# Input products of a state-space layer: three 32-row matrix products against one of 128 rows, stacked by way of DRAM

## The chip, the cores and the metric

The kernel runs on one core of one Trainium2 chip. The time is that of the device for one execution, in microseconds (us). Three runs of the kernel before took 2914.17, 2914.20 and 2915.66 us; the median is 2914.2 us.

## The reference: what is computed

The kernel computes two layers of a streaming encoder on 256 tokens of width 2048, in float32. Each layer does this:

```
h  = rms_norm(x) ;  proj = h @ w_in            # latents, u (1024 wide), gate logits
a  = mla(...)                                  # attention, 16 heads, block-causal mask
s  = s5(u, ...)                                # state-space model, 64 groups of 16 inputs and 64 states
x  = x + rms_norm((sigmoid(ga)*a + sigmoid(gb)*s) @ w_out)
x  = x + rms_norm(swiglu(rms_norm(x)))
```

The part that matters here is the entry of the state-space model. A group g has 16 input channels and 64 complex states, and its inputs are turned into state inputs by a small complex matrix:

```
bu_re = einsum('bsgp,gnp->bsgn', u, bb_re)     # (256 tokens, 16 inputs) -> 64 states, per group
bu_im = einsum('bsgp,gnp->bsgn', u, bb_im)
```

A scan over the 256 tokens follows, then the product with C, a skip term, a GELU and a gated linear layer (GLU).

## The kernel before, in words

**Products in two parts.** Tiles of type `F32R` hold one part of a number. Each operand of a big product is split into a high part and a low remainder, and the product is taken as high x high + high x low + low x high: three products where one would do. The big products (`gemm`, lines 448 to 450) do that with 128x128 weights and 512 columns. Each weight tile is loaded by a DMA of the SP queue, copied to its high part by ScalarE (line 187), and VectorE subtracts to get the low part (the tile `lo`, in `Weights.split_to`; its time shows at line 151, a helper through which all VectorE operations pass).

**Main line and background.** The program text goes through the big products of a layer one after the other: input projection (`u`, `ckv`, `cq`, `ga`, `gb`), attention, output projection `wo`, GLU, `out`, feed-forward. Everything else is background, woven in when the program is written: after each group of six matrix products (`bg.step`) the planner runs what has come due (`bg.later`, `bg.chain`: so many steps from now) and then lets the generators in its list go on, as long as the VectorE time that it has counted is less than the counted TensorE time plus a lead. So the order of instructions on each engine is fixed when the program is written. The planner's costs know nothing of how long a DMA takes.

**The state-space model (generator `s5`)** is background. It works in 32 steps `ct` of two groups each, four steps to one tile of 128 inputs (`ft`, eight tiles). For each `ft`, `prep` builds the input matrix: four ScalarE copies, two transposes on TensorE, a high part `bd[:, 0]` (ScalarE) and a low part `bd[:, 1]` (VectorE), then the same for C. For each `ct`, `emit_bu` multiplies the 32 rows that belong to its two groups: `bd[r, e, i]` against `uz[r, e, ft]`, where `uz` holds the high and low part of u, transposed. VectorE then takes the result `bu` from PSUM, scans it, and `emit_y` multiplies with C (128 rows, 32 columns). `emit_bu` for the next `ct` is due two steps after VectorE has read the last one. The state-space model starts during the input projection and has to be done when the GLU begins: `begin_glu` runs all background that is left.

**Where bu gets its operands.** Both `bd` and `uz` lie in SBUF in the places where the 32 rows of a `ct` are four different strips of the 128 partitions. `u_ready` tells the generator that half of `uz` is there (entries 1 and 2 are appended eight steps after each of the two products `u`); before `emit_bu` of the next `ct` it waits until the preparation of that `ft` has been issued (`mats[ft][2]`).

**Queues.** Weights, gates and C come by SP's queue. POOL's queue carries, in the kernel before, only the small vectors at the start, the state-space tables of the second layer and the rows of x at the two ends of a layer: nothing while the state-space steps run.

The functions that the change touches are `s5` with `prep`, `emit_bu` and the loop over `ct`, the lines after each product `u`, and the head of the loop over the layers:

Of the kernel before, what the change touches and what calls it, by code (L numbers as in the profile page):

```python
# [10 lines left out]
F32R = mybir.dt.float32r  # L11
# [9 lines left out]
S = 256  # L21
# [199 lines left out]
def trunk_kernel(ctx: ExitStack, tc: tile.TileContext, a: dict, out: bass.AP, cst: bass.AP,  # L221
                 depth: int = 2, tap=None):
    nc = tc.nc
    PE, ACT, SP = nc.tensor, nc.scalar, nc.sync
# [7 lines left out]
    dp = ctx.enter_context(tc.tile_pool(name="dp", bufs=1, space=DRAM))  # L232
# [4 lines left out]
    bg = Background()  # L237
# [3 lines left out]
    def T(pool, shape, tag, dt=F32, **kw):  # L241
        cnt[0] += 1
        return pool.tile(list(shape), dt, tag=tag, name=f"{tag}_{cnt[0]}", **kw)
# [11 lines left out]
    def tt(o, x, y, op):  # L255
        V.tensor_tensor(out=o, in0=x, in1=y, op=op)
# [10 lines left out]
    def act(o, x, f, **kw):  # L267
        ACT.activation(out=o, in_=x, func=f, **kw)  # L268
# [3 lines left out]
    def parts(hi, lo, src):  # L272
        return [lambda: act(hi, src, AF.Copy), lambda: tt(lo, src, hi.bitcast(F32), SUB)]
# [197 lines left out]
    def transpose(o, x, rows=128):  # L471
        PE.transpose(o, x, ident[0:rows, 0:rows])  # L472
# [386 lines left out]
    tab_d, base_d = T(dp, [128, 928], "tab"), T(dp, [128, 2048], "base")  # L859
    prev = ExitStack()  # L860
    for l in range(depth):
        u_ready = []
        h = feat.h
        uz = mp = sp = ap = st = sub = None

# [15 lines left out]
        def s5(l=l, gains=gains):  # L881
# [70 lines left out]
            def load_c(ft):  # L952
                t = T(sp, [128, 2, 2, 64], "craw", bufs=2)
                for i, nm in enumerate(("ssm_c_re", "ssm_c_im")):
                    src = a[nm][l, 8 * ft:8 * ft + 8].rearrange("g p n -> (g p) n")
                    for d in range(2):
                        SP.dma_start(out=t[:, i, d], in_=src)
                return t

            yps = T(ps5, [128, 2, S], "y")  # L960
            mats = {}

            def prep(ft, craw):

                bx = T(sp, [128, 2, 4, 2, 16], "bx")
                for i in range(2):
                    for g in range(2):
                        act(bx[:, i, :, g], bb[:, i, 4 * ft:4 * ft + 4], AF.Copy, scale=gm[g])
                ps = yps[:, ft % 2]
                bd = T(sp, [128, 2, 2, 128], "bd", F32R, bufs=2)  # L970
                cm = T(sp, [128, 2, 4, 2, 16], "cm", bufs=2)

                def tr(srcs):
                    for i in range(2):
                        transpose(ps[:, 128 * i:128 * i + 128], srcs[i])

                def ev_c(i):
                    v = ps[:, 128 * i:128 * i + 128].rearrange("p (c g q) -> p c g q", g=2, q=16)
                    for g in range(2):
                        act(cm[:, i, :, g], v[:, :, g], AF.Copy, scale=gm[2 * i + g])  # L980

                it = bg.chain(2, [
                    lambda: tr([bx[:, i].rearrange("p c g q -> p (c g q)") for i in range(2)]),
                    lambda: None,
                    *parts(bd[:, 0], bd[:, 1], ps.rearrange("p (i n) -> p i n", i=2)),
                    lambda: tr([craw[:, i].rearrange("p d n -> p (d n)") for i in range(2)]),
                    lambda: None, lambda: ev_c(0), lambda: ev_c(1)])
                mats[ft] = (bd, cm, it)

            def emit_bu(ct):  # L990
                ft, c = divmod(ct, 4)
                r = slice(32 * c, 32 * c + 32)
                bd = mats[ft][0]
                bu = T(ps5, [128, 2, S], "bu")
                for i in range(2):
                    o = bu[:, i]
                    uh, ul = uz[r, 0, ft], uz[r, 1, ft]
                    PE.matmul(out=o, lhsT=bd[r, 0, i], rhs=uh, start=True, stop=False)  # L998
                    PE.matmul(out=o, lhsT=bd[r, 1, i], rhs=uh, start=False, stop=False)  # L999
                    PE.matmul(out=o, lhsT=bd[r, 0, i], rhs=ul, start=False, stop=True)  # L1000
                bus[ct] = bu

            def emit_y(ct, xx):
                ft, c = divmod(ct, 4)
                cm = mats[ft][1]
                yo = yps[32 * c:32 * c + 32, ft % 2]
                for i in range(2):
                    PE.matmul(out=yo, lhsT=cm[:, i, c].rearrange("p g q -> p (g q)"), rhs=xx[:, i],  # L1008
                              start=(i == 0), stop=(i == 1))
# [21 lines left out]
            nxt_c = load_c(1)  # L1031
# [4 lines left out]
            e = e_start(0)  # L1036
# [3 lines left out]
                e_add(e, t, 0, k)  # L1040
                yield
            e_mirror(e)
            yield from bg.until(mats[0][2])
            while not u_ready:
                yield
            bu_due = bg.later(1, lambda: emit_bu(0))
            y_due = None
            yield
            for ct in range(NCT):
                ft, c = divmod(ct, 4)  # L1050
                if c == 1 and ft + 1 < 8:
                    prep(ft + 1, nxt_c)
                    if ft + 2 < 8:
                        nxt_c = load_c(ft + 2)
                yield from bg.until(bu_due)
                bu = bus.pop(ct)
                more = ct + 1 < NCT
                if more:
                    en = e_start(ct + 1)
                    et = e_mul(en, ct + 1, 0)  # L1060
                buv = bu.rearrange("p i t -> p t i")
                p1 = T(sp, [128, S, 2], "P", bufs=2)
                tt(p1, e, buv, MUL)
                p2 = T(sp, [128, S, 2], "P", bufs=2)
                tt(p2, e, buv[:, :, ::-1], MUL)
                if more:
                    e_add(en, et, ct + 1, 0)
                yield
                if more:
                    while len(u_ready) < 1 + (ct + 1) // 16:  # L1070
                        yield
                    yield from bg.until(mats[(ct + 1) // 4][2])
                    bu_due = bg.later(2, lambda ct=ct: emit_bu(ct + 1))
                z = T(sp, [128, 2, S], "Z")
                tt(z[:, 0], p1[:, :, 0], p1[:, :, 1], ADD)
                tt(z[:, 1], p2[:, :, 0], p2[:, :, 1], SUB)
                yield
                if more:
                    et = e_mul(en, ct + 1, 1)
                dec = mag[:, ct:ct + 1].to_broadcast([128, S])  # L1080
                for i in range(2):
                    V.tensor_tensor_scan(out=z[:, i], data0=dec, data1=z[:, i], initial=0.0, op0=MUL, op1=ADD)
                yield
                if more:
                    e_add(en, et, ct + 1, 1)
                zz = z.rearrange("p i t -> p t i")
                p3 = T(sp, [128, S, 2], "P", bufs=2)
                tt(p3, e, zz, MUL)
                p4 = T(sp, [128, S, 2], "P", bufs=2)
                tt(p4, e[:, :, ::-1], zz, MUL)  # L1090
                yield
                if more:
                    e_mirror(en)
                if y_due is not None:
                    yield from bg.until(y_due)
                xx = T(sp, [128, 2, S], "xx", bufs=2)
                tt(xx[:, 0], p3[:, :, 0], p3[:, :, 1], SUB)
                tt(xx[:, 1], p4[:, :, 0], p4[:, :, 1], ADD)
                yield
                y_due = bg.later(2 if more else 1, lambda ct=ct, xx=xx: emit_y(ct, xx))  # L1100
                if more:
                    e = en
                if c == 3:
                    g = T(sp, [128, 2, S], "gelu", bufs=1)
                    bg.chain(4 if more else 2, gelu(ft, g), 3 if more else 1)
# [20 lines left out]
        for c in range(2):  # L1126
            def done_u(tb, ps, c=c):
                nonlocal arena, utok
                if arena is None:
                    arena = T(xp, [128, 4096], "X")  # L1130
                    utok = arena[:, 2048:4096].rearrange("p (b n) -> p b n", b=2)
                act(utok[:, tb, 512 * c:512 * c + 512], ps, AF.Copy, scale=rstd[:, tb:tb + 1])

            gemm("u", KD, lhs_of(h), 512, done_u, before=first if c == 0 else None)
            put_pairs(3, uz, 4 * c, lambda c=c: utok[:, :, 512 * c:512 * c + 512])
            bg.later(8, lambda: u_ready.append(1))


        ckvT = T(ap, [128, 2, 2, S], "ckvT", F32R)
# [162 lines left out]
        for p in range(NPAIR):  # L1302
# [33 lines left out]
            for h_ in range(2):  # L1336
                o = kk_ps[:, 256 * h_:256 * h_ + 256]
                e = slice(256 * h_, 256 * h_ + 128)
# [14 lines left out]
            for tb in range(NT):  # L1353
                o = v_ps[:, 256 * tb:256 * tb + 256].rearrange("p (h e) -> p h e", h=2)
# [12 lines left out]
        p = NPAIR - 1  # L1367
# [142 lines left out]
```

## Time and profile before

| | |
|---|---|
| median of three runs | 2914.2 us |
| the profiled execution, its own time | 2915.5 us |
| its span, first to last instruction | 2913.7 us |
| TensorE busy | 2882.4 us (99%) |
| VectorE busy | 1902.1 us (65%) |
| ScalarE busy | 1412.6 us (48%) |
| POOL busy | 33.1 us (1%), 65 instructions |
| moved by DMA | 553.77 MB, mean 190 GB/s |
| mean granted TensorE clock | 0.998 of full speed |

PE is TensorE, PEld its weight loads, DVE VectorE, ACT ScalarE; POOL issues DMAs of its own queue. A matrix product's duration in the trace is from its issue to its last result, and the products overlap: the step from one start to the next is what a product costs the engine. A line such as `32*128 32x256` reads: a weight of 32 rows and 128 columns, and a moving operand of 32 rows and 256 columns.

### The profile page before, as it was taken

Reading aid. Unit: us, or ns where it says so; the run is one execution under the profiler, and the core shown is the slowest. Engines: PE = TensorE matmul, PEld = TensorE weight load, DVE = VectorE, ACT = ScalarE, POOL = GpSimd, SP = SyncE. Lnnn points to the kernel's source line nnn. Section 1 sums busy time; section 2 is a strip of 40 time slices with the busy share of each in tenths; the row PEclk is TensorE's granted clock in tenths of the full one; section 3 lists DMA queues with packets and bytes.
Section 4 is the critical chain, followed back from the end, with each engine's and each line's share of the span. In section 5 each row is a group of like instructions: output and inputs, shape, how many; then the busy total and the mean of one; then the engine's idle time right before and its main releaser. Section 6 shows DMA issues by size and latency. Waiting matters only on the chain.

```text
span 2913.7 us, 37400 instructions
## 1 busy us (share of the span) xinstructions
PE 2882.4 (99%) x13557; PEld 2353.5 (81%) x13557; DVE 1902.1 (65%) x2988; ACT 1412.6 (48%) x2343; POOL 33.1 (1%) x65
## 2 busy tenths in 40 slices
PE   8999999999999999999999999999999999999998
PEld 7777887788788888888877778878878888888887
DVE  7888998775665454444478888976655454544444
ACT  6655665444544444344366556644445444444433
POOL 0000000000000000000010000000000000000000
PEclk9999999999999999999999999999999999999999
DMA  7666335666666566666576663357666666666654
GB/s 225 198 195 190 111 117 177 201 223 205 211 203 212 180 189 200 190 198 199 180 228 193 198 187 112 113 174 240 225 209 209 186 188 195 188 181 231 198 198 145
DMA packets 311221, 553.77 MB, mean 190 GB/s; under 512 B 44352, under 2 KB 57084, under 8 KB 310652
## 3 DMA queue, kind: packets, MB, share of 16 engines
q1 hardware_dynamic: 301708, 528.43, 58.2%
q0 software_dynamic: 4544, 14.42, 1.5%
q10 hardware_dynamic: 4784, 8.53, 0.8%
q8 instruction: 106, 1.74, 0.2%
q14 instruction: 79, 0.65, 0.1%
HBM read 532.74 MB, written 18.56 MB: 189 GB/s over the span
## 4 chain that ended last, share of the span: by engine, by line
PE 96%; DVE 2%; DMA 1%; ACT 1%; issue 0%; DVEq 0%; ACTq 0%
PE acc L448 28%; PE acc L449 28%; PE acc L450 28%; PE y L1008 2%; PE aux L472 2%; PE bu L998 1%; PE acc L1313 1%; PE acc L1314 1%; PE acc L1315 1%; DVE lo L151 1%; DMA xo<-x 1%; PE bu L999 1%; DVE X L151 1%; PE bu L1000 1%; PE aux L1293 1%; PE aux L1244 0%
## 5 line engine op out<-in xcount | busy, mean ns | idle before, releaser
L151 DVE TENSOR_TENSOR lo<-raw,hi 128x1024 fp32r<-128x1024 f32 (+3 forms) x992 | 1147.2, 1171 | 604.0 <-PE acc L449 392.4
L187 ACT ACTIVATE hi<-raw 128x1024 fp32r<-128x1024 f32 (+3 forms) x992 | 993.8, 1019 | 731.3 <-PE acc L450 556.3
L448 PE MATMUL acc<-hi,H 128*128 128x512 f32 (+1 forms) x2432 | 965.3, 397 | 0.6 <-ACT hi L187 0.3
L450 PE MATMUL acc<-hi,H 128*128 128x512 f32 (+1 forms) x2432 | 945.6, 389 | 4.4 <-DVE H L151 4.2
L449 PE MATMUL acc<-lo,H 128*128 128x512 f32 (+1 forms) x2432 | 946.2, 389 | 1.1 <-DVE lo L151 0.9
L448 PEld LDWEIGHTS acc<-hi,H 128*128 128x128 f32 x2432 | 457.5, 188 | 108.9 <-issue 13.2
L450 PEld LDWEIGHTS acc<-hi,H 128*128 128x128 f32 x2432 | 457.6, 188 | 103.8 <-DVE H L151 8.8
L449 PEld LDWEIGHTS acc<-lo,H 128*128 128x128 f32 x2432 | 458.0, 188 | 89.4 <-DVE lo L151 2.5
L448 PE MATMUL acc<-hi,aT 128*128 128x512 f32 x704 | 274.4, 390 | 0.0
L449 PE MATMUL acc<-lo,aT 128*128 128x512 f32 x704 | 274.1, 389 | 0.0
L450 PE MATMUL acc<-hi,aT 128*128 128x512 f32 x704 | 274.1, 389 | 0.0
L448 PEld LDWEIGHTS acc<-hi,aT 128*128 128x128 f32 x704 | 132.2, 188 | 27.6
L449 PEld LDWEIGHTS acc<-lo,aT 128*128 128x128 f32 x704 | 132.2, 188 | 27.4
L450 PEld LDWEIGHTS acc<-hi,aT 128*128 128x128 f32 x704 | 132.2, 188 | 27.1
L448 PE MATMUL acc<-hi,uz 128*128 128x512 f32 x256 | 101.2, 396 | 1.6 <-ACT uz L268 1.6
L268 ACT ACTIVATE X<-acc,rstd 128x512 f32<-128x512 f32 (+1 forms) x64 | 41.2, 650 | 122.0 <-PE acc L450 119.5
L448 PE MATMUL acc<-hi,mT 128*128 128x512 f32 x256 | 100.2, 391 | 0.0
L449 PE MATMUL acc<-lo,uz 128*128 128x512 f32 x256 | 100.0, 390 | 0.2 <-DVE lo L151 0.2
L450 PE MATMUL acc<-hi,uz 128*128 128x512 f32 x256 | 99.8, 390 | 0.0
L450 PE MATMUL acc<-hi,mT 128*128 128x512 f32 x256 | 99.7, 390 | 0.0
L449 PE MATMUL acc<-lo,mT 128*128 128x512 f32 x256 | 99.7, 389 | 0.0
L268 ACT ACTIVATE aT<-aux 128x512 fp32r<-128x512 f32 x44 | 26.1, 599 | 146.4 <-PE aux L472 146.4
(194 smaller groups left out, 2707.0 us busy)
## 6 DMA issues: line engine op xcount, KB each, us to landing
raw<-in_w_in_dram SPq DMA_DIRECT2D x176, 512.0 KB, 4.3
raw<-in_w_ffn_gate_dram SPq DMA_DIRECT2D x176, 512.0 KB, 4.2
raw<-in_w_ffn_up_dram SPq DMA_DIRECT2D x176, 512.0 KB, 3.8
raw<-in_w_ffn_down_dram SPq DMA_DIRECT2D x176, 512.0 KB, 4.5
raw<-in_w_o_mla_dram SPq DMA_DIRECT2D x64, 512.0 KB, 4.2
raw<-in_w_glu_dram SPq DMA_DIRECT2D x64, 512.0 KB, 4.8
raw<-in_w_out_dram SPq DMA_DIRECT2D x64, 512.0 KB, 4.7
raw<-in_w_uq_dram SPq DMA_DIRECT2D x32, 384.0 KB, 3.5
```

What stands on the lines that cost most here:

```text
L151: return f(**kw)
L187: self.nc.scalar.activation(out=dst(hv), in_=src(self.raw[n]), func=AF.Copy)
L268: ACT.activation(out=o, in_=x, func=f, **kw)
L448: PE.matmul(out=o, lhsT=xh, rhs=h[:, kk], start=(k == 0), stop=False)
L449: PE.matmul(out=o, lhsT=xh, rhs=lo[:, kk], start=False, stop=False)
L450: PE.matmul(out=o, lhsT=xl, rhs=h[:, kk], start=False, stop=(k == nk - 1))
L472: PE.transpose(o, x, ident[0:rows, 0:rows])
L998: PE.matmul(out=o, lhsT=bd[r, 0, i], rhs=uh, start=True, stop=False)
L999: PE.matmul(out=o, lhsT=bd[r, 1, i], rhs=uh, start=False, stop=False)
L1000: PE.matmul(out=o, lhsT=bd[r, 0, i], rhs=ul, start=False, stop=True)
L1008: PE.matmul(out=yo, lhsT=cm[:, i, c].rearrange("p g q -> p (g q)"), rhs=xx[:, i], start=(i == 0), stop=(i == 1))
L1293: PE.matmul(out=o[:, 256 * h_:256 * h_ + 256], lhsT=t["v"][:, 0, e], rhs=pT[:, h_, 0:256], start=True, stop=False)
```

## The change: what it does

The four blocks of 32 rows that make up a product in two parts are stacked over the 128 partitions: matrix `bs` holds [high, low, high, low] of B, operand `us` holds [high, high, low, low] of u. One product of 128 rows then gives high x high + low x high + high x low + low x low. The stacks are made by way of DRAM: u goes to `u_d` (two DMAs of 512 KB for each half, `put_u`, eight steps after each product `u`), each prepared B goes to `b_d[ft]` (one DMA of 256 KB, `put_b`, a step in the middle of `prep`'s chain), and `load_stacks` reads them back. A stack serves two `ct` (a pair `p`); it takes eight DMAs of 64 KB, four for `bs` and four for `us`, each onto 32 partitions. There are two buffers of each; the stack of pair p+2 is issued when `emit_bu` has used pair p, and no earlier than the `b_d` and `u_d` that it reads. All of these DMAs are issued from POOL. `bd` has one buffer in place of two. `prep(ft + 1)` is called late in the first `ct` of a tile, not at the start of the second. The generator waits for the stack of the next pair to have been issued, not for `mats[ft]`.

```diff
-        u_ready = []
+        u_ready, more_u = [], []
+        u_d = T(dp, [2, 128, 8, S], f"u_d{l}", F32R)
+
+        def put_u(c):
+            for e in range(2):
+                nc.gpsimd.dma_start(out=u_d[e, :, 4 * c:4 * c + 4], in_=uz[:, e, 4 * c:4 * c + 4])
+            u_ready.append(1)
+            for f in more_u:
+                f()
...
-                bd = T(sp, [128, 2, 2, 128], "bd", F32R, bufs=2)
+                bd = T(sp, [128, 2, 2, 128], "bd", F32R)
...
                     *parts(bd[:, 0], bd[:, 1], ps.rearrange("p (i n) -> p i n", i=2)),
+                    lambda: put_b(ft, bd),
...
+            b_d = T(dp, [8, 2, 128, 2 * 128], f"b_d{l}", F32R)
+            stacks, nput = {}, [0]
+
+            def put_b(ft, bd):
+                nc.gpsimd.dma_start(out=b_d[ft].rearrange("e p n -> p e n"), in_=bd.rearrange("p e i n -> p e (i n)"))
+                nput[0] = ft + 1
+                load_stacks()
+
+            def load_stacks():
+                while len(stacks) < 2 + len(used) and len(stacks) < 2 * nput[0] and len(stacks) < 8 * len(u_ready):
+                    p = len(stacks)
+                    ft, c0 = divmod(p, 2)
+                    rows = slice(64 * c0, 64 * c0 + 64)
+                    bs = T(sp, [128, 2, 256], "bs", F32R, bufs=2)
+                    us = T(sp, [128, 2, S], "us", F32R, bufs=2)
+                    for e in range(4):
+                        for dst, src in ((bs, b_d[ft, e % 2, rows]), (us, u_d[e // 2, rows, ft])):
+                            nc.gpsimd.dma_start(out=dst[32 * e:32 * e + 32], in_=src.rearrange("(c r) n -> r c n", r=32))
+                    stacks[p] = (bs, us)
...
             def emit_bu(ct):
-                ft, c = divmod(ct, 4)
-                r = slice(32 * c, 32 * c + 32)
-                bd = mats[ft][0]
+                p, c = divmod(ct, 2)
+                bs, us = stacks[p]
                 bu = T(ps5, [128, 2, S], "bu")
                 for i in range(2):
-                    o = bu[:, i]
-                    uh, ul = uz[r, 0, ft], uz[r, 1, ft]
-                    PE.matmul(out=o, lhsT=bd[r, 0, i], rhs=uh, start=True, stop=False)
-                    PE.matmul(out=o, lhsT=bd[r, 1, i], rhs=uh, start=False, stop=False)
-                    PE.matmul(out=o, lhsT=bd[r, 0, i], rhs=ul, start=False, stop=True)
+                    PE.matmul(out=bu[:, i], lhsT=bs[:, c, 128 * i:128 * i + 128], rhs=us[:, c], start=True, stop=True)
                 bus[ct] = bu
+                if c == 1:
+                    used.append(p)
+                    load_stacks()
...
-            yield from bg.until(mats[0][2])
-            while not u_ready:
+            yield from bg.until(mats[0][1])
+            while not stacks:
                 yield
...
-                if c == 1 and ft + 1 < 8:
-                    prep(ft + 1, nxt_c)
...
-                    while len(u_ready) < 1 + (ct + 1) // 16:
+                    while (ct + 1) // 2 not in stacks:
                         yield
-                    yield from bg.until(mats[(ct + 1) // 4][2])
...
+                if c == 0 and ft + 1 < 8:
+                    prep(ft + 1, nxt_c)
...
-            bg.later(8, lambda: u_ready.append(1))
+            bg.later(8, lambda c=c: put_u(c))
```

## Rows read from the trace of the kernel before

**Rows 1.** The page's first part: busy time, share of the span, instructions.
```profile
PE 2882.4 (99%) x13557; PEld 2353.5 (81%) x13557; DVE 1902.1 (65%) x2988; ACT 1412.6 (48%) x2343; POOL 33.1 (1%) x65
```
**Rows 2.** The chain that ended last, share of the span by engine.
```profile
PE 96%; DVE 2%; DMA 1%; ACT 1%; issue 0%; DVEq 0%; ACTq 0%
```
**Rows 3.** Timeline of PE, one bu block: start, duration, line, tiles, rows*columns.
```profile
109.42 0.39 PE L450 MATMUL acc<-hi,H 128*128 128x512 f32 x1
109.74 0.38 PE L998 MATMUL bu<-uz,bd 32*128 32x256 f32 x1
109.96 0.27 PE L999 MATMUL bu<-uz,bd 32*128 32x256 f32 x1
...
110.42 0.27 PE L1000 MATMUL bu<-uz,bd 32*128 32x256 f32 x1
110.63 0.50 PE L448 MATMUL acc<-hi,H 128*128 128x512 f32 x1
110.96 0.40 PE L449 MATMUL acc<-lo,H 128*128 128x512 f32 x1
111.20 0.39 PE L450 MATMUL acc<-hi,H 128*128 128x512 f32 x1
```
**Rows 4.** Groups by line: busy us, mean ns, and idle time before.
```profile
L151 DVE TENSOR_TENSOR lo<-raw,hi 128x1024 fp32r<-128x1024 f32 (+3 forms) x992 | 1147.2, 1171 | 604.0 <-PE acc L449 392.4 <-ACT hi L187 145.2 <-issue 59.6
L998 PE MATMUL bu<-uz,bd 32*128 32x256 f32 x128 | 42.1, 329 | 0.0
```
**Rows 5.** Timeline of PE in attention: 128-row products of 256 columns, then a block.
```profile
313.66 0.28 PE L1313 MATMUL acc<-cqT,hi 128*128 128x256 f32 x1
313.78 0.28 PE L1314 MATMUL acc<-cqT,lo 128*128 128x256 f32 x1
313.90 0.28 PE L1315 MATMUL acc<-cqT,hi 128*128 128x256 f32 x1
314.11 0.38 PE L998 MATMUL bu<-uz,bd 32*128 32x256 f32 x1
```
**Rows 6.** Busy time by stretch (all engines), then line 998 alone in the attention stretches.
```profile
150.00:310.00 160.00, 160.00 (x709) 121.20 (x708) 132.61 (x219) 84.92 (x181) 0.00 (x0) 1.00 0.64 186
312.00:432.00 120.00, 120.00 (x835) 106.91 (x833) 111.30 (x269) 83.49 (x246) 0.00 (x0) 1.00 0.34 104
1780.00:1890.00 110.00, 109.66 (x764) 98.15 (x762) 102.12 (x248) 75.28 (x228) 0.00 (x0) 1.00 0.33 105
325.00:345.00 20.00, 20.00 (x143) 17.77 (x142) 19.27 (x49) 14.96 (x53) 0.00 (x0) 1.00 0.26 85
...
312.00:432.00 120.00, 5.92 (x18) 3.29 (x18) 1.00 0.34 104
1780.00:1890.00 110.00, 5.26 (x16) 2.92 (x16) 1.00 0.33 105
```
**Rows 7.** DMA issues: tile, queue, count, KB each, median us to landing.
```profile
x<-X POOLq DMA_DIRECT2D x24, 256.0 KB, 5.1
xo<-x POOLq DMA_DIRECT2D x16, 256.0 KB, 5.2
nat<-in_pre_ffn_norm_dram POOLq DMA_DIRECT2D x1, 8.0 KB, 4.8
par<-in_ssm_a_re_dram POOLq DMA_DIRECT2D x1, 16.0 KB, 5.5
ldt<-in_ssm_log_dt_dram POOLq DMA_DIRECT2D x1, 0.2 KB, 5.6
```
**Rows 8.** Timeline of POOL at a layer's boundary, and busy time of that stretch.
```profile
1457.56 0.54 POOL L696 DMA_DIRECT2D x<-X  x1
1458.09 0.55 POOL L690 DMA_DIRECT2D xo<-x  x1
1458.63 0.54 POOL L696 DMA_DIRECT2D x<-X  x1
...
1457.00:1474.00 17.00, 15.71 (x75) 11.78 (x74) 14.61 (x34) 10.44 (x28) 6.48 (x12) 1.00 0.84 255
```
**Rows 9.** Timeline, low part of B ready (DVE) and first bu that needs it (PE), both layers.
```profile
85.99 0.41 DVE L151 TENSOR_TENSOR bd<-y,bd 128x256 fp32r<-128x256 f32 x1
105.89 0.38 PE L998 MATMUL bu<-uz,bd 32*128 32x256 f32 x1
...
1512.89 0.42 DVE L151 TENSOR_TENSOR bd<-y,bd 128x256 fp32r<-128x256 f32 x1
1519.13 0.38 PE L998 MATMUL bu<-uz,bd 32*128 32x256 f32 x1
...
1762.98 0.42 DVE L151 TENSOR_TENSOR bd<-y,bd 128x256 fp32r<-128x256 f32 x1
1785.58 0.38 PE L998 MATMUL bu<-uz,bd 32*128 32x256 f32 x1
...
1864.24 0.40 DVE L151 TENSOR_TENSOR bd<-y,bd 128x256 fp32r<-128x256 f32 x1
1901.63 0.38 PE L998 MATMUL bu<-uz,bd 32*128 32x256 f32 x1
```
**Rows 10.** Busy time by stretch at a layer's boundary: PE first, granted clock third from last.
```profile
730.00:740.00 10.00, 7.23 (x35) 5.43 (x36) 9.26 (x16) 6.35 (x17) 2.71 (x6) 1.00 0.92 311
740.00:750.00 10.00, 10.00 (x40) 8.07 (x39) 5.89 (x18) 7.55 (x15) 0.19 (x1) 0.83 0.48 150
```

More of the change, by code (lines that the diff above doesn't have):

```diff
@@ L985, in prep @@
                     *parts(bd[:, 0], bd[:, 1], ps.rearrange("p (i n) -> p i n", i=2)),
+                    lambda: put_b(ft, bd),
                     lambda: tr([craw[:, i].rearrange("p d n -> p (d n)") for i in range(2)]),
                     lambda: None, lambda: ev_c(0), lambda: ev_c(1)])
-                mats[ft] = (bd, cm, it)
+                mats[ft] = (cm, it)
+            b_d = T(dp, [8, 2, 128, 2 * 128], f"b_d{l}", F32R)
[4 more added lines that the diff above has]
+                load_stacks()
@@ L990, in emit_bu @@
+            used = []
+            more_u.append(load_stacks)
             def emit_bu(ct):
-                ft, c = divmod(ct, 4)
-                r = slice(32 * c, 32 * c + 32)
-                bd = mats[ft][0]
+                p, c = divmod(ct, 2)
+                bs, us = stacks[p]
                 bu = T(ps5, [128, 2, S], "bu")
                 for i in range(2):
-                    o = bu[:, i]
-                    uh, ul = uz[r, 0, ft], uz[r, 1, ft]
-                    PE.matmul(out=o, lhsT=bd[r, 0, i], rhs=uh, start=True, stop=False)
-                    PE.matmul(out=o, lhsT=bd[r, 1, i], rhs=uh, start=False, stop=False)
-                    PE.matmul(out=o, lhsT=bd[r, 0, i], rhs=ul, start=False, stop=True)
+                    PE.matmul(out=bu[:, i], lhsT=bs[:, c, 128 * i:128 * i + 128], rhs=us[:, c], start=True, stop=True)
@@ L1001, in emit_bu @@
                 bus[ct] = bu
+                if c == 1:
+                    used.append(p)
+                    load_stacks()
             def emit_y(ct, xx):
                 ft, c = divmod(ct, 4)
-                cm = mats[ft][1]
+                cm = mats[ft][0]
                 yo = yps[32 * c:32 * c + 32, ft % 2]
@@ L1050, in s5 @@
                 ft, c = divmod(ct, 4)
-                if c == 1 and ft + 1 < 8:
-                    prep(ft + 1, nxt_c)
-                    if ft + 2 < 8:
-                        nxt_c = load_c(ft + 2)
                 yield from bg.until(bu_due)
@@ L1095, in s5 @@
                     yield from bg.until(y_due)
+                if c == 0 and ft + 1 < 8:
+                    prep(ft + 1, nxt_c)
+                    if ft + 2 < 8:
+                        nxt_c = load_c(ft + 2)
                 xx = T(sp, [128, 2, S], "xx", bufs=2)
```

## The prediction

> **What bounds the kernel now.** Three views, in this order. The page's first part shows TensorE busy for 99% of the span, VectorE for 65%, POOL for 1% [rows 1]. The chain of waits that ended last is 96% TensorE [rows 2]. So a microsecond taken from TensorE's list is a microsecond of the result, unless another engine takes its place in that stretch. The third view, busy time by stretch, tells where that could be: while the state-space steps run beside the projections, VectorE is busy 132.6 of 160 us (83%); beside attention 111.3 of 120 and 102.1 of 110 (both 93%) [rows 6]. The change works only in these stretches.
>
> **What it removes.** A bu block is six products of 32 rows. Its cost is read from starts, not from durations, since products overlap. From the last big product before the block (109.42) to the second one after it (110.96) is 1.54 us [rows 3]; I read all 64 blocks (128 first products, two to a block [rows 4]), and those between big products take 1.54 to 1.57 but for two of 1.39. Of it the six steps inside are 0.11 to 0.12 us each, apart from the first, 0.22; the way in is 0.32 where a big product otherwise starts 0.23 after the last (109.19 to 109.42 in the trace, likewise 110.96 to 111.20 [rows 3]), and the big product behind the block is followed after 0.33, not 0.23. So there are six products and a loss at each change of shape.
>
> **What it adds on TensorE.** Two products of 128 rows and 256 columns. The same shape and type stands in attention: starts 313.66, 313.78, 313.90, 0.12 us apart [rows 5]. A block becomes 2 x 0.12 = 0.24 us, and with the big product before and the one behind at 0.23 each the distance is 0.70 in place of 1.55: 0.85 us saved. In attention, from 313.90 through the block the same sum gives 0.85 as well. 64 x 0.85 = 54.4 us. Bounds: if the loss at the change of shape stayed, only four products of 0.115 go, 64 x 0.46 = 29.4 us; above it I see nothing more than 56.
>
> **What it adds on POOL and the queues.** Per layer: four DMAs of 512 KB for u, eight of 256 KB for B, 16 x 8 = 128 of 64 KB for the stacks; 280 issues in both. A POOL issue takes 0.54 us and the next starts right behind [rows 8]; 280 x 0.54 = 151 us on an engine that is idle there. Bytes: per layer 2 + 2 written, 8.4 read back, some 25 MB on 554. SP's queue is passed by none of it, and its own share in these stretches is 0.64 and less [rows 6]. I set both at zero; if weights came later because of them, ScalarE's high copies would be late next.
>
> What has a price is the path from a finished B to its first product, which before was nothing. It runs: `put_b` from issue to landing 5.1 us (as x<-X, also 256 KB out of SBUF); then, behind that wait, eight loads, the last issued 7 x 0.54 = 3.8 us after the first; and its landing, 5.5 us (par and ldt; the larger xo has 5.2, and the first of the small vectors 4.8) [rows 7, 8]. Sum 14.4 us from the end of B's low part. No row shows loads of 32 partitions in pieces of 1 KB written as F32R, so I keep 10 us (landings of 4, loads in parallel) and 25 us (both landings doubled) as ends.
>
> Against that stands the slack, from the end of the low part to the first product that needs it [rows 9]:
> - First tile of layer 1: 86.40 to 105.89, 19.5 us. Covered, 5 us to spare. (It is E and not B that is late there, so the extra link in `prep`'s chain costs nothing.)
> - First tile of layer 2: 1513.31 to 1519.13. The chain's extra link moves the product one step, six times 0.23 = 1.4 us, to 1520.5. The stack lands at 1513.31 + 14.4 = 1527.7: TensorE stands for **7.2 us**. In its list, the rest of the input projection is queued behind that product, and on VectorE the low parts of weights stand behind the read of bu, so nothing is caught up. Ends: 3 and 18.
> - The other 14 tiles: 22.2 to 37.0 us, mean 27.1 over all of them; the tightest and the last are shown. With TensorE faster by 0.85 in some 13.4 us per step, 6%, the tightest is 20.9. Covered by 6 us; at the 25 end the sum over the 14 is 17 us.
> - Loads of every second stack wait only for the buffer: about 10 us in the 27 us of two steps.
>
> A stand of that length has its own cost: where TensorE worked 7.23 of 10 us, the next 10 us ran at a granted clock of 0.83 [rows 10], so part of it at the lower of the two levels (1.2 in place of 2.4 GHz). I take the same 10 x 0.17 = **1.7 us**; ends 0 and 4.
>
> `emit_bu` now waits for eight DMAs in place of engines. Waits that are long fulfilled cost before nothing that I can see; as an end, 0.05 us for each on TensorE's list would be 32 x 8 x 0.05 = 13 us. I take 0. The earlier `prep` moves four ScalarE copies and two transposes by a step or so, and `bd` with one buffer waits for a DMA that landed long ago: 0.
>
> **What VectorE takes back.** The attention stretches hold 9 and 8 blocks (18 and 16 first products). Shortened by 7.7 and 6.8 us they are 112.3 and 103.2 us long, with 111.3 and 102.1 us of VectorE work: 99% [rows 6]. Nearest row: at 19.27 of 20 us (96%) TensorE still worked all 20. Of 14.5 us saved there I take **4** as lost (ends 0 and 14.5). In the other stretches 83% becomes 88%: nothing.
>
> **Sum**, on the profiled execution's own 2915.5 us (span 2913.7 and 1.8 around it): 2915.5 - 54.4 + 7.2 + 1.7 + 4 = 2874.0, or 41.5 us less. The median of the runs is 1.3 us lower, so 2914.2 - 41.5 = 2872.7; I say 2873.
>
> **A rule that speaks against it.** Rows first: POOL's issues stayed at 0.54 to 0.55 us where VectorE was busy 14.6 of 17 us, and their landings at 5.1 and 5.2 [rows 7, 8]. The Trainium skill, SBUF — State Buffer, section "SBUF: two separate sides", says that descriptors of a DMA issued from GpSimd can't be written while VectorE runs an operation in a two-port mode; its figures, 620 ns alone and some 3100 ns beside a copy, would add 2.5 us to each issue and, by the sum of rival 3, end near 3070 us (an estimate from that page). The trace does not bear it out for the operations of a layer's boundary; the state-space steps' own operations are not shown beside a POOL issue, so a form of it stands as rival 3.
>
> **Rivals.**
> 1. *No stand, nothing taken back*: stacks land sooner and VectorE keeps up. 2914.2 - 54.4 = 2860. For it: TensorE idles nowhere at 96% VectorE. Against: 5.8 us of slack against any chain of DMAs at the start of layer 2. Chance 15%.
> 2. *Gain eaten by more of the same*: loss at the change of shape kept, or VectorE the bound beside attention, with waits on TensorE's list. From 2873: + 25 for the first (54.4 - 29.4), or + 10.5 + 13 for the others. About 2897. For it: 93% in rows 6. Against: no loss between products of 512 and of 256 columns of full shape is seen inside attention. Chance 22%.
> 3. *POOL's issues are held* (the other side). Each of the nine issues in the path waits for VectorE's running operation and gets through late by x. The path is 14.4 + 9x. At x = 1.17, one low-part subtraction [rows 4], it is 24.9 us: 17 us over the 14 tiles, 10.5 more at layer 2's start, 5 at layer 1's, end 2905. At twice that (2.34) the path is 35.5: 140 + 21 + 16 = 177 us more, 3050. It turns into a loss from x = 1.25, an issue of 1.8 us. For it: nine issues in a row, and VectorE at 83 to 93%. Against: rows 8. Loads that can't be in flight together act alike. Chance of x over 1.25: 12%; near it: 4%.
> 4. *It doesn't do what it says*: the stack lacks a term or waits are wrong. The diff's blocks [h,l,h,l] by [h,h,l,l] give all products; nothing in rows speaks for it. Within rival 3.
>
> **How the numbers follow.** Forecast 47% (its own range 2863 to 2888), rival 1 15%, rival 2 22%, rival 3 16%. What a measurement here tells from no change is some 0.2%, 6 us. Faster by more: 47 + 15 + 22 - 1 = 83%. Within: 5%. Slower: 12%. The range runs from rival 1's end, 2858, to 2903, which leaves out rival 3's loss and a little on either side.
>
> **What would show it.** Right: block distance of about 0.70 us at each of the 64; one stand of TensorE of 5 to 10 us at the first bu of layer 2, none at the first of layer 1; POOL at some 345 issues of 0.54 us; VectorE near 99% beside attention. Wrong: TensorE waiting for `bs` or `us` at each fourth step; POOL issues over 1.8 us; landings of 10 us; a gap at each block in spite of the full shape.

## The result, and the profile after

The changed kernel takes 2883.2 us (four runs, 2882.5 to 2884.6) against 2914.2: ratio 0.9891, 95% interval 0.9879 to 0.9903. That is 31.1 us less; the forecast was 41.5 less. The profiled execution took 2884.6 us, its span is 2882.8.

The page's first part and the head of the chain of waits, changed kernel (columns as in [rows 1, 2]):

```profile
PE 2835.1 (98%) x13301; PEld 2326.1 (81%) x13301; DVE 1901.4 (66%) x2988; ACT 1411.7 (49%) x2343; POOL 184.1 (6%) x345
...
PE 92%; DVE 3%; DMA 2%; issue 1%; ACT 1%; SPq 0%; DVEq 0%; ACTq 0%; POOL 0%; POOLq 0%
```

TensorE's busy time fell by 47.3 us, 16 us more than the span: the rest came back as waits. TensorE's share of the chain fell from 96 to 92%. Its busy time also holds products that ran slowly; the clock is looked at below.

The timeline of TensorE around one block, changed kernel, first layer (the two products stand in one row, `x2`):

```profile
110.76 0.39 PE L450 MATMUL acc<-hi,H 128*128 128x512 f32 x1
110.99 0.40 PE L1031 MATMUL bu<-us,bs 128*128 128x256 f32 x2
111.22 0.40 PE L448 MATMUL acc<-hi,H 128*128 128x512 f32 x1
111.45 0.40 PE L449 MATMUL acc<-lo,H 128*128 128x512 f32 x1
```

From the last big product before the block to the second one after it: 111.45 - 110.76 = 0.69 us, where [rows 3] have 1.54. So the saving per block is the forecast's 0.85 us. Read over all 64 blocks, the distance is 0.69 to 0.71 us between big products (before: 1.54 to 1.57 but for two) and 0.46 to 0.61 elsewhere (before: 1.28 to 1.44), all but three: 0.78, 0.96, and the one with the stand told below. What TensorE waited for, changed kernel (total us, times, longest):

```profile
PE aux L472 <- DVE X L151: 7.3, 6, 2.0
PE bu L1031 <- DMA bs<-b_d: 6.7, 1, 6.7
PE y L1042 <- DVE bd L151: 6.4, 3, 3.1
...
PE acc L448 <- ACT X L268: 1.1, 2, 0.9
...
PE y L1042 <- ACT cm L268: 0.9, 1, 0.9
```

The same view of the kernel before has 7.4 us in the first line, 0.2 in the fourth, and none of the other three. So two waits are new: the one that was foreseen, for `bs`, once; and one that was not, y for `bd` (with one for `cm` beside it). The second is told first.

**y waits for the next tile's B.** Timelines of TensorE, VectorE and TensorE again, changed kernel, beside attention:

```profile
316.32 0.38 PE L472 MATMUL y<-cs,bx 128*128 128x128 f32 x2
...
323.58 0.42 DVE L151 TENSOR_TENSOR bd<-y,bd 128x256 fp32r<-128x256 f32 x1
...
324.05 1.05 PE L1042 MATMUL y<-xx,cm 128*32 128x256 f32 x4 [2.52 <-DVE bd L151]
...
334.08 1.05 PE L1042 MATMUL y<-xx,cm 128*32 128x256 f32 x4 [0.92 <-ACT cm L268]
...
1519.02 1.05 PE L1042 MATMUL y<-xx,cm 128*32 128x256 f32 x4 [0.79 <-DVE bd L151]
...
1780.55 1.92 PE L1042 MATMUL y<-xx,cm 128*32 128x256 f32 x4 [3.12 <-DVE bd L151]
```

The tile `y` has two halves in PSUM: y of the current tile of inputs is summed in one, the transposes of the next tile's B and C are put into the other. In the kernel before, y of a tile's first step stands in TensorE's list ahead of the transposes of B. TensorE's timeline, kernel before:

```profile
332.41 1.05 PE L1008 MATMUL y<-xx,cm 128*32 128x256 f32 x4
333.39 0.44 PE L472 MATMUL y<-cs,bx 128*128 128x128 f32 x2
```

With `prep` called a step earlier the transposes (316.32) come first, and the y behind them starts when the last reader of the other half, the low part on VectorE, has ended (324.00). The four waits make 7.4 us. That it is the shared tile which makes y wait is read from this order and the kernel's text; two separate tiles were not tried.

**The start of layer 2.** Timelines of VectorE, POOL and TensorE, changed kernel:

```profile
1491.69 0.42 DVE L151 TENSOR_TENSOR bd<-y,bd 128x256 fp32r<-128x256 f32 x1
...
1492.40 0.71 POOL L1006 DMA_DIRECT2D b_d<-bd  x1 [10.92 <-DVE bd L151]
1497.01 0.56 POOL L1020 DMA_DIRECT2D bs<-b_d  x1 [3.90 <-DMA b_d<-bd]
...
1500.71 0.53 POOL L1020 DMA_DIRECT2D us<-u_d  x1
...
1505.60 0.77 PE L1031 MATMUL bu<-us,bs 128*128 128x256 f32 x2 [6.71 <-DMA bs<-b_d]
```

Busy time by stretch behind it, changed kernel (granted clock third from last):

```profile
1505.00:1510.00 5.00, 4.40 (x17) 4.43 (x18) 3.59 (x8) 2.08 (x4) 4.29 (x9) 0.50 0.58 145
1510.00:1515.00 5.00, 5.00 (x33) 4.99 (x33) 5.00 (x9) 2.54 (x8) 0.00 (x0) 0.91 0.94 279
```

From the end of the low part (1492.11): 0.3 to the issue of `put_b`, 4.6 to its landing, 3.7 for seven issues, 4.9 to the first product: 13.5 us, forecast 14.4. The stretch from 1505 to 1510 us, in which the stand ends, ran at 0.50, which is the lower level, 1.2 GHz, and the next at 0.91: by these two rows at most 5 x 0.50 + 5 x 0.09 = 3.0 us.

**The stack loads.** The summary of the tile `bs`, changed kernel: its POOL instructions (duration min/median/max in ns, first and last start) and the landing of its DMAs:

```profile
L1020 POOL DMA_DIRECT2D bs<-b_d x128: 532/536/607, 96.5 to 1851.4; - x128
...
DMA to landing us min/median/max: 2.1/4.4/7.8
```

The summary of line 1031 on TensorE, with the waits ahead of it (us, times), changed kernel:

```profile
L1031 PE MATMUL bu<-us,bs x128: 277/282/550, 108.0 to 1916.2; 128*128 128x256 f32 x128
its engine sat idle before it (us, times) until:
  DMA bs<-b_d: 6.7, 1
```

Busy time in a stretch beside attention, changed kernel (POOL's is the one ahead of the clock):

```profile
310.00:430.00 120.00, 116.56 (x798) 104.74 (x797) 112.46 (x267) 83.36 (x241) 18.32 (x34) 1.00 0.47 133
```

An issue takes 0.54 us at the median and 0.61 at most (0.72 for `put_b`), also beside attention with VectorE at 112.46 of 120 us (18.32 us for 34 issues). One of the 128 products waited.

### The profile page after: what moved, and what is told of

It is laid out like the page before. It is cut to its first block, busy times and chain, and to the rows that moved or that the text cites. A ratio compares the mean times of both kernels' runs of the same rounds, so it can differ in the third digit from the quotient of the medians.

```text
span 2882.8 us, 37387 instructions
## 1 busy us (share of the span) xinstructions
PE 2835.1 (98%) x13301; PEld 2326.1 (81%) x13301; DVE 1901.4 (66%) x2988; ACT 1411.7 (49%) x2343; POOL 184.1 (6%) x345
## 4 chain that ended last, share of the span: by engine, by line
PE 92%; DVE 3%; DMA 2%; issue 1%; ACT 1%; SPq 0%; DVEq 0%; ACTq 0%; POOL 0%; POOLq 0%
PE acc L448 27%; PE acc L450 27%; PE acc L449 27%; PE y L1042 2%; PE aux L472 2%; DVE lo L151 1%; DMA raw<-in_w_in_dram 1%; DMA xo<-x 1%; PE acc L1346 1%; PE acc L1347 1%; PE acc L1348 1%; PE bu L1031 1%; DVE X L151 1%; PE aux L1326 0%; PE aux L1277 0%
```

## The experiments

Nine kernels ran, in the order below. The medians of the kernel before in the same comparisons were 2914.5 to 2915.1 us. Differences from the kernel before are against these; those from the changed kernel are against its 2883.2 us, measured beside a kernel before of 2914.2.

**1. `prep` back.** The changed kernel, with `prep(ft + 1)` called where it was before the change; the load of C for the tile after that goes with it.

```diff
+                if c == 1 and ft + 1 < 8:
+                    prep(ft + 1, nxt_c)
...
-                if c == 0 and ft + 1 < 8:
-                    prep(ft + 1, nxt_c)
...
```

> The changed kernel with one part undone: prep of the next tile is called again at the start of the second ct, as before the change. The changed kernel takes 2883.2 us. Theory A (the moved prep sets a new wait: the C product y of the first ct now comes behind the transposes of B in TensorE's list and waits until VectorE has taken the low part of B): the four waits of y for bd and cm (2.52 and 0.92 us in layer 1, 0.79 and 3.12 us in layer 2, 7.4 us in all) go, and the waits of the transposes for ScalarE at 117 us (1.0 us) as well; 2875 to 2877 us. Theory B (VectorE is full beside attention, 99% after the shortening, and the wait of y is only where that shows): the same microseconds are lost in other places, 2881 to 2884 us. The wait of the first bu of layer 2 for its stack stays at 6 to 8 us in both.

Measured: 2876.2 us (2873.7 to 2878.3), ratio 0.9868 (0.9851 to 0.9884), 7.0 us less than the changed kernel. TensorE's timeline, `prep` back, the same y as above and the first product of layer 2:

```profile
321.59 1.05 PE L1042 MATMUL y<-xx,cm 128*32 128x256 f32 x4
322.57 0.44 PE L472 MATMUL y<-cs,bx 128*128 128x128 f32 x2
...
1503.64 0.77 PE L1031 MATMUL bu<-us,bs 128*128 128x256 f32 x2 [6.83 <-DMA bs<-b_d]
```

y stands ahead of the transposes again and waits for nothing; the stand stays. So in the changed kernel the moved `prep` costs about what its waits come to (7.0 us against 7.4).

**2. All u loads of a pair first.** If the seven issues set the stand, it shrinks when u, which is in DRAM earlier, no longer stands between the loads of B.

```diff
-                    for e in range(4):
-                        for dst, src in ((bs, b_d[ft, e % 2, rows]), (us, u_d[e // 2, rows, ft])):
-                            nc.gpsimd.dma_start(out=dst[32 * e:32 * e + 32], in_=src.rearrange("(c r) n -> r c n", r=32))
+                    for dst, at in ((us, lambda e: u_d[e // 2, rows, ft]), (bs, lambda e: b_d[ft, e % 2, rows])):
+                        for e in range(4):
+                            nc.gpsimd.dma_start(out=dst[32 * e:32 * e + 32], in_=at(e).rearrange("(c r) n -> r c n", r=32))
```

> The changed kernel with the eight loads of a stack in another order: the four of u first, then the four of B. The path from a finished B to its first product then holds four issues behind the landing of b_d, not eight: 4 x 0.53 = 2.1 us less. Theory A (that path is what TensorE waits for at the start of layer 2): the wait there falls from 6.7 to about 4.6 us, the stretch at the lower clock is as long or shorter; 2880 to 2881.5 us, from 2883.2. Rival (TensorE waits there for the u stack or for landings that take as long in any order): the wait stays at 6 to 7 us and the time within 1 us of 2883.2.

Measured: 2882.5 us (2880.6 to 2883.6), ratio 0.9891 (0.9876 to 0.9905): nothing. A miss. The product and the wait ahead of it, TensorE's timeline of this version:

```profile
1506.09 0.76 PE L1031 MATMUL bu<-us,bs 128*128 128x256 f32 x2 [6.56 <-DMA us<-u_d]
```

POOL's timeline at that place, this version:

```profile
1493.75 2.14 POOL L1020 DMA_DIRECT2D us<-u_d  x4
1497.89 2.10 POOL L1020 DMA_DIRECT2D bs<-b_d  x4 [2.00 <-DMA b_d<-bd]
```

Landing of these four loads of `us`, then of these four of `bs`:

```profile
DMA to landing us min/median/max: 4.8/6.3/6.7
...
DMA to landing us min/median/max: 5.4/6.5/7.0
```

All four of `us` have landed by 1502.0; the last of `bs`, issued at 1499.46, lands at 1505.8, 0.3 us ahead of the product. So the product waits for B, as theory A says; the `us` that the profile names belongs to the next stack, whose first load lands at 1505.99. In the changed kernel too the last load of the stack (issued at 1500.71) lands 0.3 us ahead of the product, at 1505.3. What the edit saves in issues comes back in landing: the last load takes 6.3 us to land where it took 4.6. So a landing is no fixed price that can be added behind the issues, as theory A did. Why the loads land later was not tried by itself.

**3. First pair of layer 2 as before.** The first two steps of layer 2 keep the six products of 32 rows and need no stack; `bd` has two buffers. The core of the edit:

```diff
...
+                if p == 0 and l > 0:
+                    r, bd0 = slice(32 * c, 32 * c + 32), bds[0]
+                    for i in range(2):
+                        for j, (eb_, eu) in enumerate(((0, 0), (1, 0), (0, 1))):
+                            PE.matmul(out=bu[:, i], lhsT=bd0[r, eb_, i], rhs=uz[r, eu, 0], start=(j == 0), stop=(j == 2))
+                else:
...
```

> The changed kernel, but in layer 2 the first two ct take B and u from where they lie, with the six products of 32 rows each, and only pairs from the second on come by way of DRAM (bd has two buffers again). Theory A (the start of layer 2 costs the 6.7 us that TensorE stands, some 2.6 us at the lower clock behind it): no wait at the first bu of layer 2 and full clock there, 9.3 us less, and 2 x 0.7 us more for the two blocks of six: 2875 to 2877 us. Rival (the stand hides a wait for weights that comes then anyway): 2880 to 2884 us, with TensorE waiting for low parts or weights in the same 40 us.

Measured: 2880.4 us (2874.5 to 2881.9), ratio 0.9880 (0.9866 to 0.9895), 2.8 us less than the changed kernel. The wait for `bs` is gone, but the waits of y for `bd` grew. Waits of TensorE, this version:

```profile
PE y L1049 <- DVE bd L151: 10.0, 3, 4.4
```

The longest of the three, in its timeline:

```profile
1515.59 0.62 PE L1049 MATMUL y<-xx,cm 128*32 128x256 f32 x2 [4.40 <-DVE bd L151]
```

Busy time by stretch at that place, this version (granted clock third from last):

```profile
1515.00:1520.00 5.00, 4.41 (x13) 2.79 (x14) 4.93 (x11) 3.29 (x10) 0.71 (x1) 0.66 0.75 203
```

With TensorE earlier at the first tile, its y comes to the next tile's low part earlier too: 4.4 us where the changed kernel waits 0.8, and the clock falls behind this wait instead. Of the 9.7 us that the stand and its slow stretch come to, 1.7 go on the two blocks of six, 3.6 on longer waits of y, and some 1.7 (5 x 0.34) on the lower clock: 2.7 are left, near the 2.8 measured (an estimate; this run's interval is some 4 us to either side). The two waits are in part one behind the other, so neither edit alone shows what it is worth.

**4. Both.** Edits 1 and 3 together.

> Both at once: prep called where it was before the change, and the first pair of layer 2 straight from SBUF. If the two losses are independent (theory A for both) the gains add: 2883.2 - 7 - 8 = 2867 to 2870 us. If VectorE is the bound (theory B) only the second is gained: 2875 to 2877 us.

Measured: 2870.7 us (2870.4 to 2871.0), ratio 0.9851 (0.9836 to 0.9866). 12.5 us less than the changed kernel, more than 7.0 + 2.8, and 0.7 above theory A's range. With `prep` back, what edit 3 saves is no longer taken by the wait of y.

**5. `prep` moved alone.** The kernel before, with only the call of `prep` (and the load of C with it) moved as in the change.

> The kernel before (2914.5 us), with one part of the change alone: prep of the next tile is called late in the first ct, ahead of its xx, as in the changed kernel; the six products and no DRAM trip. Theory A (the moved call by itself puts the C product of the first ct behind the transposes of B and makes it wait for VectorE's low part): TensorE waits of 1 to 4 us at the y of single tiles, above all beside attention and in the first tile of layer 2, 5 to 9 us in all, 2919 to 2923 us. Theory B (the waits need a TensorE that runs ahead of VectorE, as it does only when the products are shorter): within 2 us of 2914.5.

Measured: 2923.3 us (2919.8 to 2927.7), ratio 1.0030 (1.0020 to 1.0039): 8.2 us slower (5.8 to 11.4 by the interval), 0.3 above theory A's range. TensorE's waits in it, of which the kernel before has neither:

```profile
PE y L1008 <- DVE bd L151: 4.2, 2, 2.5
...
PE y L1008 <- ACT bd L268: 1.5, 1, 1.5
```

They make 5.7 us. The profiled execution is 7.7 us longer than that of the kernel before; of this, 1.7 are there at TensorE's 31st product (17.7 us from the start, 16.0 in the kernel before), long before the first `prep` that was moved.

**6. Products alone.** The kernel before, where two products of 128 rows take `bd` and `uz` as they lie. They are not the right blocks: bu and all behind it have other values; shapes, places and counts are those of the change, without the trip through DRAM.

```diff
-                    PE.matmul(out=o, lhsT=bd[r, 0, i], rhs=uh, start=True, stop=False)
-                    PE.matmul(out=o, lhsT=bd[r, 1, i], rhs=uh, start=False, stop=False)
-                    PE.matmul(out=o, lhsT=bd[r, 0, i], rhs=ul, start=False, stop=True)
+                    PE.matmul(out=bu[:, i], lhsT=bd[:, i, i], rhs=uz[:, i, ft], start=True, stop=True)
```

> The kernel before with the products alone changed: two of 128 rows and 256 columns for each ct, straight from bd and uz as they lie, no stacks and no DRAM trip (left out: the groups aren't kept apart and the low x high terms are missing, so only the time counts). If the sum of the prediction holds, 64 x 0.85 = 54.4 us go: 2860 us, and beside attention the 9 blocks of layer 1 give all of 9 x 0.85 = 7.7 us. Theory B (VectorE is full beside attention at 99%) gives 4 to 7 us less of a gain: 2864 to 2867 us, with TensorE waiting for VectorE there.

Measured: 2864.1 us (2862.5 to 2866.5), ratio 0.9827 (0.9813 to 0.9840): 51.1 us less. The distances around the 64 blocks, added up, fall from 94.8 to 39.9 us, by 54.9: that is the sum of the prediction, 54.4. The time lies at the edge of theory B's range, but its waits are few: of the 3.3 that are missing to 54.4, the profile shows 1.6 as waits of y (1.1 for `bd`, beside attention, of which the kernel before has none, and 0.8 for `xx`, later, of which it has 0.3), and another 1.2 us are there 16 us from the start. The interval, 46.6 to 54.5 us less, does not part the two theories; the blocks' sum speaks for the first. Waits of TensorE, this version:

```profile
PE y L472 <- DVE bd L151: 1.1, 1, 1.1
...
PE y L1003 <- DVE xx L151: 0.8, 1, 0.8
```

**7. Trip alone.** The kernel before, with all DMAs to DRAM and back issued as in the change and read by nobody.

> The kernel before with the DRAM trip alone: u and B are written to DRAM and all stacks are loaded, at the same points as in the changed kernel, but nothing reads the stacks; the six products and prep stay as they were. The prediction set this traffic (25 MB, 280 issues on POOL) at nothing: 2914 to 2916 us. Rival (the rest that is missing, some 7 us in the version with both repairs, is traffic that makes weights late where the queues are full: around 75 to 130 us and 1480 to 1520 us): 2918 to 2922 us, with ScalarE's copies waiting longer for weights there.

Measured: 2918.5 us (2916.1 to 2922.4), ratio 1.0012 (1.0003 to 1.0021): 3.4 us slower (0.9 to 6.1 by the interval), small but not nothing, and in the rival's range. Busy time by stretch where the first stacks load, of this version (DMA share second from last; 0.65 in the same stretch of the kernel before):

```profile
75.00:130.00 55.00, 54.83 (x258) 43.75 (x257) 47.09 (x97) 38.03 (x81) 9.90 (x18) 1.00 0.82 226
```

The DMA engines are busier there, but TensorE loses only 0.2 us. The wait that the kernel before has not comes in layer 2. Timelines of ScalarE, VectorE (two rows) and TensorE, this version:

```profile
1537.45 1.06 ACT L187 ACTIVATE hi<-raw 128x1024 fp32r<-128x1024 f32 x1 [2.63 <-DMA raw<-in_w_in_dram]
...
1539.29 0.35 DVE L151 SCALAR_TENSOR_TENSOR E<-E,seeds,Et 128x128 f32<-128x128 f32 x1 [2.92 <-ACT Et L268]
...
1541.94 0.42 DVE L151 TENSOR_TENSOR bd<-y,bd 128x256 fp32r<-128x256 f32 x1
...
1542.41 0.44 PE L472 MATMUL y<-cs,craw 128*128 128x128 f32 x2 [1.98 <-DVE bd L151]
```

ScalarE stands for a late weight, what it does for the state-space model comes later, so does VectorE's low part of B, and TensorE's transposes of C stand for that. ScalarE's waits for weights of the input projection, kernel before and then this version:

```profile
ACT hi L187 <- DMA raw<-in_w_in_dram: 22.7, 21, 4.8
...
ACT hi L187 <- DMA raw<-in_w_in_dram: 56.7, 37, 5.0
```

So the rival holds: the traffic goes with later weights, and in this execution TensorE loses 2.0 us by it. The rest of the 3.4 is not shown to be the trip's: this execution was 1.4 us behind that of the kernel before already 16 us from the start, ahead of the first DMA of the trip (46.8 us).

**8. and 9. Hold the first product.** Full products everywhere, `prep` back, and the first block of layer 2 placed 7 and then 14 steps later in TensorE's list in place of 1. If the stand is a matter of place in the list, it goes; if the time is only put off, it comes back at the GLU.

```diff
-            bu_due = bg.later(1, lambda: emit_bu(0))
+            bu_due = bg.later(14 if l > 0 else 1, lambda: emit_bu(0))
...
```

> The changed kernel with `prep` back at the start of the second step of a tile, and the first input product of layer 2 woven in seven steps after its stack is issued instead of one. All 64 blocks are full products. Theory A (the stand is a matter of place in TensorE's list: the projection's products queue behind a product whose operands are 13 us away; six steps of about 1.4 us are 8.4 us against a stand of 6.8): no wait for `bs` over 1 us, granted clock 1.00 between 1500 and 1515 us, and 5 to 8 us less than the version with `prep` back alone (2876.2), that is 2868 to 2871, some 1 to 2 us below the version with six 32-row products in the first two blocks (2870.7) since two blocks more are short. Rival B (the 8 us are only moved: the state-space steps start that much later and have to be done when the GLU begins, so TensorE stands there or VectorE is late beside attention): the wait for `bs` goes, but waits of the same sum appear at the start of the GLU, time 2875 or more.

> As the run before it, which held the first product of layer 2 for seven steps (2874.2 us; TensorE still stood 3.9 us at that product, as the steps there are products of 320 columns and shorter than I reckoned), but held for fourteen. Theory A (place in the list): the wait for `bs` is gone, clock 1.00 from 1500 to 1515 us, 3.9 us of stand and some 1.5 of lower clock come back, 2868 to 2871. Rival B (the hold starts the state-space steps later, and what is saved in front is lost behind: waits of y for ACT's `cm` have come to 3.9 us in the run before, 0.2 with `prep` back alone): wait for `bs` gone, but waits of y and at the start of the GLU grow, 2873 or more.

Measured: with 7 steps 2874.2 us (2873.7 to 2877.8), ratio 0.9861 (0.9844 to 0.9877), a miss: TensorE still waits 3.9 us for `bs` (the six steps there were shorter than I had reckoned), as well as, in its profiled execution, 3.9 us for `cm` and 1.2 us at the first product of layer 1, where the slack was 5 us by the prediction. With 14 steps 2868.1 us (2866.6 to 2869.5), ratio 0.9839 (0.9823 to 0.9856). TensorE's first block of layer 2, 14 steps:

```profile
1506.73 0.40 PE L1031 MATMUL bu<-us,bs 128*128 128x256 f32 x2
```

Busy time by stretch at that place and beside attention, 14 steps:

```profile
1500.00:1505.00 5.00, 5.00 (x27) 4.19 (x26) 2.16 (x2) 3.71 (x8) 2.71 (x5) 1.00 1.23 287
1505.00:1510.00 5.00, 5.00 (x26) 4.19 (x25) 3.56 (x9) 2.69 (x9) 0.00 (x0) 1.00 1.24 321
...
310.00:430.00 120.00, 119.44 (x808) 107.06 (x808) 115.18 (x270) 85.35 (x249) 18.41 (x34) 1.00 0.50 141
```

The block comes 1.1 us later than in the changed kernel, but TensorE has worked up to it, at full clock; no wait came up at the GLU. Of the waits of y, 1.2 us for `cm` and 0.8 for `xx` are left. This is the fastest of the versions that compute the reference, 15.1 us below the changed kernel and 46 to 47 below the kernel before. From version 4 its interval does not part it. From the changed kernel it differs by one number and one place of a call, and by no data path.

## Why the prediction was right, and where it was short

The sign, the two main terms (the block and the stand) and the range (2858 to 2903) held; the time came out 10.4 us above the forecast. That it still fell into the range is in part luck: the range's width was there for other terms, and none of it was there for a wait of y. The parts, each measured by itself:

| part | forecast, us | measured, us | from |
|---|---|---|---|
| products, with what VectorE takes back | -54.4 + 4 = -50.4 | -51.1 | run 6 |
| first product of layer 2, with the clock | 7.2 + 1.7 = 8.9 | 8.1 | run 1 less run 9 |
| `prep` moved | 0 | 7.0 and 8.2 | changed kernel less run 1; run 5 |
| trip through DRAM | 0 | 3.4 | run 7 |
| sum | -41.5 | -32.6 to -31.4 | |
| the change | | -31.1 | |

The parts add up to the change within 1.5 us, closer than their intervals (3 to 5 us to either side) can show, and the two that I set to zero make up the miss.

- **The step that failed** is "The earlier `prep` moves four ScalarE copies and two transposes by a step or so [...]: 0". I looked at what the moved chain itself waits for and at the buffer of `bd`, not at who stands behind it on TensorE. The transposes passed one item of TensorE's list, y of the first step, and in the four waits y began only when the transposes' last reader, on VectorE or ScalarE, was through: 0.8 to 3.1 us each, 7.0 to 8.2 us by the runs' times. The kernel's text gave the hint: `prep` and `emit_y` write the same tile. The order of before was to be had from its trace.
- **Traffic at zero** was the second, smaller miss: 25 MB cost 3.4 us with nobody waiting for them, of which the trace shows 2.0, as a weight that came late. What would be late next was named in the prediction, ScalarE's high copies; its price was set at zero from the DMA share in the mean (0.64 and less).
- **The block**: 0.85 us, 54.9 in all, as forecast. Its waits for eight DMAs cost nothing when long fulfilled, as I took it: 0.69 us per block in the changed kernel and in run 6, which loads no stacks. VectorE's share beside attention is another matter. I forecast 99% and 4 us lost; it was 112.46 of 120 us, 94%, in the changed kernel, and with the waits of y for `bd` gone (run 9) 115.18, 96%, with TensorE at 119.44. In run 6 at most 3.3 us of the whole are missing, 1.6 of them waits of y, and no queue of attention's own work is seen. So the 4 us are not borne out, and that 50.4 and 51.1 lie so near is luck. Rival 2's loss at the change of shape did not come.
- **The stand**: one, at the place named, 6.7 us against 7.2; the path was 0.9 us shorter. No wait at layer 1, none at the 14 other tiles, as the slack said. The clock fell to the lower level from 1505 to 1510 us; by the rows that cost at most 3.0 us in the changed kernel and some 1.4 (5 x 0.27) in run 1, where 1.7 was forecast. The path's parts did not add up as I thought: run 2 cut four issues from it and the landings grew. Not foreseen was that run 3's way of removing the stand hands half of it on to y.
- **Rival 3** (POOL's issues held by VectorE) is dead: the loads' issues took 0.61 us at most where 1.8 were needed, and 34 issues took 18.32 us with VectorE busy 94% of the stretch. The rule of the Trainium skill, SBUF — State Buffer, section "SBUF: two separate sides", speaks of operations in a two-port mode, and the same section says that `tensor_tensor` has none; of VectorE's 675 operations from 108 to 500 us in the changed kernel 418 are `tensor_tensor`. So the prediction's 3070 us applied the rule to work most of which the section leaves out, and no run here was made to test it.
- **Rival 1** was near for the version of run 9 (2868.1, forecast for no stand and nothing taken back 2860); what parts them is the trip's 3.4 and the products' missing 3.3 us, 6.7 of 8.1.

Open: what the trip costs beyond the 2.0 us shown, why the loads of run 2 land later, and whether y would wait if its two halves were two tiles. The last was not tried.

## What to carry to other kernels

When a step of background work is called earlier, list for each engine the instructions that it passes, and ask of each whether it writes a buffer that the moved step now holds: the cost is not in what moved but in what it moved ahead of. A product that needs a trip through DRAM (13 us here) belongs that far behind its operands in the list; here a place further back did it (run 9), and the one try at a shorter trip did not (run 2). Two edits that each remove one of two waits on one list can show half their worth alone. Measure the parts alone and see whether they add up.

## What the runs showed that I had not expected

- Six products of 32 rows and 256 columns cost 1.55 us per block with the ways in and out, two of 128 rows 0.70 with the same big products around them; the six steps inside are no shorter than those of 128 rows. So here the rows cost nothing: of the 0.85 us, four steps of 0.115 make 0.46, and the rest, by subtraction, goes with the change of shape there and back.
- A stand of 6.7 us ended in a stretch of five microseconds at a granted clock of 0.50 in the changed kernel, and in the version with `prep` back a stand of 6.83 was followed by five at 0.73:

```profile
1505.00:1510.00 5.00, 5.00 (x28) 5.00 (x28) 5.00 (x12) 3.38 (x7) 1.71 (x4) 0.73 0.85 259
```

  That is a mean between the two levels. Taking away this stand with its slow stretch (run 9) gave back 8.1 us, 1.3 more than the stand itself.
- Loads of `bs`, 64 KB each, issued one after another from POOL, land after 2.1 to 7.8 us, median 4.4: the same kind of transfer differs nearly fourfold. What makes the difference no run here shows.
